# A one-core hybrid decoder trunk: every fourth weight piece's low part is subtracted on GpSimd, with five pairs of piece buffers in place of four

## The chip, the cores and the metric

The kernel runs on one core of one Trainium2 chip. A core has five engines with queues of their own: TensorE (PE in the profile, its weight loads PEld), VectorE (DVE), ScalarE (ACT), GpSimd (POOL) and SyncE (SP), which here issues all DMAs. The metric is the device time of one execution in microseconds (us); lower is better.

## The reference

Two decoder layers run over 256 tokens of width 2048, all in float32. Layer 0 mixes tokens by an eight-head retention, layer 1 by a short gated convolution, and each layer ends with a SwiGLU feed-forward block of width 5632. Scales, shifts and gates of every block come from a conditioning vector c.

```python
c_act = jax.nn.silu(c)
for i in range(DEPTH):                       # DEPTH = 2
    mod = (c_act @ w_mod[i] + b_mod[i])[:, None, :]
    sh1, sc1, g1, sh2, sc2, g2 = jnp.split(mod, 6, axis=-1)
    h = rms_norm(x, norm1_g[i]) * (1.0 + sc1) + sh1
    y = retention_mixer(h, ...) if i == 0 else short_conv_mixer(h, ...)
    x = x + g1 * y
    h = rms_norm(x, norm2_g[i]) * (1.0 + sc2) + sh2
    a, b = jnp.split(h @ ffn_w_in[i], 2, axis=-1)
    x = x + g2 * ((jax.nn.silu(a) * b) @ ffn_w_out[i])
return rms_norm(x, final_g)
```

Nearly all of the work is in the products with the weights: `ret_w_in` (2048 x 12288), `ret_w_out` (4096 x 2048), `conv_w_in` (2048 x 6144), `conv_w_out` (2048 x 2048), and twice `ffn_w_in` (2048 x 11264) and `ffn_w_out` (5632 x 2048).

## The kernel before, in words

**Split products.** Every float32 product is made of three matmuls in a shorter float32 form (fp32r): a value is written as a high part `hi` (a rounded copy) and a low part `lo` (the value less `hi`), and hi x hi, hi x lo and lo x hi are summed in PSUM. Where weights are the stationary side (`product`, lines 447 and 450) the first two of these go in one matmul of 512 columns, the third is one of 256. Where the tokens are the stationary side (`thrice`, lines 460 to 462, used by `by_token` and `sevens`) there are three matmuls of 512 columns.

**Blocks and pieces.** The host lays all weights out in `w_all`, in the order of use, as 456 blocks of 128 x 2048 float32 (1 MB). `fetch` (line 370) issues one DMA on SP into one of `RAW_BUFS = 3` raw buffers; the 192 modulation rows of `w_mod` go through buffers too, most of them through the same three. `prepare` (line 376) makes one piece of a block ready: ScalarE casts the piece to `hi` (line 402), then VectorE subtracts to get `lo` (line 405). An ordinary block has two pieces of 1024 columns, piece 0 (first half) and piece 1 (second half). In the last feed-forward block some pairs of row tiles are multiplied with seven products in place of eight (class `Seven`, function `sevens`). Such a block has four pieces, numbered 2 to 5; VectorE also makes differences of weights for them (lines 391, 395 and 397), and piece 5 is only 512 columns wide. There are 996 pieces in all.

**Who sets the order.** `take` (line 410) hands the next 128 or 512 columns of a piece to the matmuls. When it begins a piece, it drops the one before and calls `prepare` until the piece in use and `AHEAD` further ones are ready in program order (`AHEAD + 1` in the last feed-forward block, line 1394). `hi` and `lo` have `PART_BUFS = 4` buffers each, so the cast of a piece waits until TensorE has finished the piece four before it. The order on TensorE is the program's own. In the start, up to the end of the first spans of the retention input, VectorE and ScalarE follow the program too; after that a scheduler orders VectorE, ScalarE, GpSimd and SP by priorities and estimated times. `units[0]` counts the 128 x 128 weight tiles used so far, in the steps in which `paced` is called; `early` (line 337) is its value behind those first spans.

**Other work beside it.** VectorE also reduces each modulation row against c (lines 318 and 755), adds up and gates the results, and builds the normalised rows of `h` as pairs of high and low parts. GpSimd has only tiny operations: it adds the bias to the modulation results (lines 323 to 328) and takes the power of the mean squares for the norms (line 546) and at the end (lines 1220 to 1222 and 1256).

**Stages**, by the profile's time: retention input and heads to about 780 us, feed-forward of layer 0 to about 1500, convolution to about 1880, the last feed-forward block to the end. The seven-product blocks begin at about 1937 us.

Of the kernel before, what the change touches and what calls it, by code (L numbers as in the profile page):

```python
# [10 lines left out]
F32 = mybir.dt.float32  # L11
# [3 lines left out]
ALU = mybir.AluOpType  # L15
# [26 lines left out]
LAST_TILES = 20, 24  # L42
STORE_AT, LOAD_AT = 0, 2
LEAD_RET, LEAD_CONV, LEAD_FFN = 6, 4, 2
AHEAD = 2
MOD_LEAD = 64
MOST = 0.045
MOD_PRIO = -300
STEPS = (8, 8, 20)
RAW_BUFS = 3  # L50
PART_BUFS = 4
LEFT, ENDS, EARLIER = 8, 2, 120

Q0, K0, V0, G0 = 0, HEADS * DK, 2 * HEADS * DK, 2 * HEADS * DK + HEADS * DV
# [202 lines left out]
def trunk(ctx: ExitStack, tc: tile.TileContext, x_in, c_in, pos_in, w_mod, cols_in, gain_in, tab_in, w_all, out):  # L257
    nc = tc.nc
    const = ctx.enter_context(tc.tile_pool(name="const", bufs=1))
    work = ctx.enter_context(tc.tile_pool(name="work", bufs=2))  # L260
    wpool = ctx.enter_context(tc.tile_pool(name="wpool", bufs=PART_BUFS))
    ps = ctx.enter_context(tc.tile_pool(name="ps", bufs=8, space=PSUM))
# [3 lines left out]
    def name(s):  # L266
        serial[0] += 1
        return f"{s}_{serial[0]}"
# [68 lines left out]
    early = sum(g.n * len(g.ks) for g in RET_SPANS)  # L337
    plan_mod = [(early, 0), (1024, 18), (1984, 49), (5184, n_mod)]
    units, allowed = [0], [0.0]
# [30 lines left out]
    def fetch():  # L370
        raw = wpool.tile([P, CHUNK], F32, tag="raw", name=name("raw"), bufs=RAW_BUFS)
        nc.sync.dma_start(raw, w_all[n_fetched[0]])
        n_fetched[0] += 1
        fetched.append(raw)

    def prepare(between=None):
        if prepared[0] == len(pieces):
            return
        _, piece = pieces[prepared[0]]
        prepared[0] += 1  # L380
        if piece in (0, 2):
            if not fetched:
                fetch()
            raws[:] = [fetched.pop(0)]
            while first <= units[0] < early and len(fetched) < RAW_BUFS - 1 and n_fetched[0] < w_all.shape[0]:
                fetch()
        whole = raws[0]
        b = [whole[:, i : i + DV] for i in range(0, CHUNK, DV)]
        raw = whole[:, :HALF] if piece in (0, 4) else whole[:, HALF:]
        if piece == 2:  # L390
            nc.vector.tensor_tensor(differences, whole[:, DV : 3 * DV], whole[:, : 2 * DV], op=ALU.subtract)
        elif piece == 3:
            raw = differences
        elif piece == 4:
            nc.vector.tensor_tensor(b[1], b[2], differences[:, :DV], op=ALU.subtract)
        elif piece == 5:
            nc.vector.tensor_tensor(b[3], b[3], b[1], op=ALU.subtract)
            raw = b[3]
        width = raw.shape[1]
        hi = wpool.tile([P, HALF], F32R, tag="hi", name=name("hi"))[:, :width]  # L400
        lo = wpool.tile([P, HALF], F32R, tag="lo", name=name("lo"))[:, :width]
        nc.scalar.copy(hi, raw)  # L402
        if between:
            between()
        nc.vector.tensor_tensor(lo, raw, hi.bitcast(F32), op=ALU.subtract)  # L405
        ready.append((hi, lo, width))

    prepared, ahead_now = [0], [AHEAD]

    def take(group, k, col, width=P):  # L410

        assert order.pop() == (group, k, col, width)
        i = place[0] or 0
        if i == 0:
            if place[0] == 0:
                ready.pop(0)
            while len(ready) < 1 + ahead_now[0] * (units[0] >= first):
                n = len(ready)
                prepare()
                if len(ready) == n:  # L420
                    break
        place[0] = (i + width) % ready[0][2]
        return [t[:, i : i + width] for t in ready[0][:2]]
# [255 lines left out]
    with ExitStack() as inner:  # L679
# [64 lines left out]
        with tc.tile_pool(name="start", bufs=1) as sp:  # L744
# [59 lines left out]
            with tc.manual_schedule(engines={mybir.EngineType.DVE, mybir.EngineType.Activation}):  # L804
# [61 lines left out]
                def before(k):  # L866
                    low = []
                    prepare(lambda: low.append(row(k)))
                    low[0]()

                pts = packed(RET_SPANS[0], h, before=before, between=both_reduced, banks=banks)
                prepare()
                prepare()
                for i, pt in enumerate(pts):
# [283 lines left out]
    def made_in_sums():  # L1158

        tmp("beside_sums", (P, BESIDE_SUMS), bufs=1)  # L1160
        for tag, n in (("u", 3), ("low", 3), ("sum", 4)):
            single_sums.extend(tmp(tag, (P, 2, P), F32R, bufs=n) for _ in range(n))
        for i in IN_SEVEN:
            both = tmp("u512", (P, 2, S), pool=mpool, bufs=3)
            for n in range(2):
                k = 2 * i + n
                high, low = [h[k].bitcast(F32)[:, v, :] for v in range(2)]
                nc.vector.tensor_tensor(both[:, n, :], high, low, op=ALU.add)
            in_sums[i] = [single_sums.pop() for _ in range(3)]
            tokens_sums_of(*parts(both), h[2 * i][:, :, P:], in_sums[i])  # L1170
# [217 lines left out]
    for part in range(2):  # L1388
        n = LAST_TILES[part] // 2
        mid = mids(LAST_TILES[part]) if part else first_mid  # L1390
        if not part:
            first_rows(mid[-2:])
            made_in_sums()
            ahead_now[0] = AHEAD + 1
        for i, groups in enumerate(LAST_IN[part]):
# [43 lines left out]
```

## Time and profile before

| what | value |
| --- | --- |
| time, median of 3 runs | 2592.86 us (2591.23 to 2596.55) |
| span of the profiled execution | 2591.5 us; the profile gives no other time for it, so what lies around the span is read from the runs: their median is 1.4 us longer |
| busy: TensorE, VectorE, ScalarE, GpSimd | 2563.3, 2197.4, 1306.0, 125.9 us |
| low-part subtractions on VectorE | 996 (912 + 42 of 1024 columns, 42 of 512) |
| clock granted to TensorE, mean | 0.998 of full speed |
| DMA | 689.56 MB, 266 GB/s on average |

How to read it: a row of the profile names the line of the kernel, the engine, the operation, its output and inputs by tile name (`lo<-raw,hi`), and the shapes. Busy time counts an engine as busy while any of its instructions is under way. Behind a bar or in brackets stands how long the engine idled before the instruction and which instruction ended that idle time. TensorE's matmuls overlap, and their ends are modelled. Spans on GpSimd are rough.

### The profile page before, as it was taken

What the parts mean: (1) busy time and instruction counts of PE and PEld (TensorE: products, weight loads), DVE (VectorE), ACT (ScalarE), POOL (GpSimd) and SP (SyncE); (2) the same over time, 40 slices, a digit from 0 to 9 for tenths busy, and PEclk for the clock granted to TensorE, in tenths of its full rate; (3) what the DMA queues carried; (4) which work ended last, traced back from release to release, by engine and by line L of the source; (5) the groups of instructions that cost most, each with busy time, mean ns of one, the idle gap of its engine ahead of it and who ended that gap; (6) DMA issues with size and microseconds to landing.
All of it is one profiled execution on the core that took longest, in us unless ns stands there. A gap on an engine that the chain in (4) does not pass through costs nothing.

```text
span 2591.5 us, 36408 instructions
## 1 busy us (share of the span) xinstructions
PE 2563.3 (99%) x14181; PEld 2236.3 (86%) x14181; DVE 2197.4 (85%) x2762; ACT 1306.0 (50%) x1792; POOL 125.9 (5%) x232
## 2 busy tenths in 40 slices
PE   7999999999999999999999999999999999999998
PEld 6898889888889888888888898888998888888887
DVE  7988978787698887777778889988989998999978
ACT  5544543444456545334444454444565554556554
POOL 0000000110000000100001001000000000000001
PEclk9999999999999999999999999999999999999999
DMA  9975768767676888777877768877845565555654
GB/s 398 388 293 209 268 243 306 300 248 277 251 282 246 330 323 307 301 296 298 298 294 283 298 237 313 330 297 277 308 165 210 188 223 205 180 210 187 222 208 147
DMA packets 96688, 689.56 MB, mean 266 GB/s; under 512 B 10737, under 2 KB 12161, under 8 KB 13441
## 3 DMA queue, kind: packets, MB, share of 16 engines
q1 hardware_dynamic: 96514, 687.23, 71.3%
q8 instruction: 111, 1.82, 0.3%
q14 instruction: 63, 0.52, 0.1%
HBM read 685.08 MB, written 2.11 MB: 265 GB/s over the span
## 4 chain that ended last, share of the span: by engine, by line
PE 94%; DVE 3%; DMA 2%; issue 1%; ACT 1%; ACTq 0%; POOLq 0%; POOL 0%; DVEq 0%
PE bank L447 30%; PE bank L450 16%; PE bank L461 12%; PE bank L460 12%; PE bank L462 12%; PE bank L495 2%; PE bank L496 2%; PE bank L494 2%; PE bank L627 1%; PE bank L629 1%; PE bank L628 1%; DVE raw L755 1%; DMA raw<-w_all 1%; DVE lo L405 1%; PE bank L983 1%
## 5 line engine op out<-in xcount | busy, mean ns | idle before, releaser
L402 ACT CAST hi<-raw 128x1024 fp32r<-128x1024 f32 (+1 forms) x954 | 978.9, 1033 | 1015.8 <-PE bank L447 346.4
L405 DVE TENSOR_TENSOR lo<-raw,hi 128x1024 fp32r<-128x1024 f32 (+1 forms) x954 | 1133.9, 1197 | 322.6 <-ACT hi L402 317.3
L447 PE MATMUL bank<-h,hi 128*128 128x512 f32 x2016 | 699.3, 390 | 0.0
L450 PE MATMUL bank<-h,lo 128*128 128x256 f32 x2016 | 568.5, 282 | 0.0
L447 PEld LDWEIGHTS bank<-h,hi 128*128 128x128 f32 x2016 | 378.4, 188 | 79.2
L460 PE MATMUL bank<-hi,h 128*128 128x512 f32 x1032 | 405.0, 392 | 2.2 <-DVE rm L739 2.2
L461 PE MATMUL bank<-lo,h 128*128 128x512 f32 x1032 | 404.3, 392 | 0.0
L462 PE MATMUL bank<-hi,h 128*128 128x512 f32 x1032 | 402.7, 390 | 0.0
L450 PEld LDWEIGHTS bank<-h,lo 128*128 128x128 f32 x2016 | 381.0, 189 | 0.1
L318 DVE SCALAR_TENSOR_TENSOR raw<-raw,cb 128x2048 f32<-128x2048 f32 x160 | 365.5, 2284 | 15.7 <-DMA raw<-w_mod 15.3
L447 PE MATMUL bank<-mid,hi 128*128 128x512 f32 x922 | 319.8, 390 | 0.0
L450 PE MATMUL bank<-mid,lo 128*128 128x256 f32 x922 | 260.1, 282 | 0.4 <-DVE lo L405 0.4
L460 PEld LDWEIGHTS bank<-hi,h 128*128 128x128 f32 x1032 | 194.4, 188 | 40.7 <-DVE rm L739 2.8
L462 PEld LDWEIGHTS bank<-hi,h 128*128 128x128 f32 x1032 | 194.2, 188 | 40.8
L461 PEld LDWEIGHTS bank<-lo,h 128*128 128x128 f32 x1032 | 194.5, 188 | 40.4 <-DVE lo L405 3.3
L447 PEld LDWEIGHTS bank<-mid,hi 128*128 128x128 f32 x922 | 173.1, 188 | 36.2
L450 PEld LDWEIGHTS bank<-mid,lo 128*128 128x128 f32 x922 | 174.2, 189 | 0.7 <-DVE lo L405 0.7
L447 PE MATMUL bank<-rm,hi 128*128 128x512 f32 x496 | 172.5, 390 | 0.0
L496 PE MATMUL bank<-h,lo 128*128 128x256 f32 x512 | 146.4, 286 | 4.6 <-DVE lo L405 4.6
L494 PE MATMUL bank<-h,hi 128*128 128x256 f32 x512 | 146.1, 285 | 3.4 <-ACT h L783 3.4
L495 PE MATMUL bank<-h,hi 128*128 128x256 f32 x512 | 146.1, 285 | 0.7 <-DVE h L784 0.7
L450 PE MATMUL bank<-rm,lo 128*128 128x256 f32 x496 | 139.8, 282 | 0.0
(256 smaller groups left out, 3197.4 us busy)
## 6 DMA issues: line engine op xcount, KB each, us to landing
raw<-w_all SPq DMA_DIRECT2D x456, 1024.0 KB, 4.8
raw<-w_mod SPq DMA_DIRECT2D x192, 1024.0 KB, 5.2
x<-x_in SPq DMA_DIRECT2D x4, 512.0 KB, 5.3
out<-xt SPq DMA_DIRECT2D x4, 512.0 KB, 3.0
decay<-tab_in SPq DMA_DIRECT2D x8, 128.0 KB, 2.4
x<-gate_row SPq DMA_DIRECT2D x2, 512.0 KB, 4.8
last_gain<-gain_in SPq DMA_DIRECT2D x1, 1024.0 KB, 7.2
cols<-cols_in SPq DMA_DIRECT2D x1, 152.0 KB, 8.3
```

Source lines behind the costliest of these rows:

```text
L318: nc.vector.scalar_tensor_tensor(raw, raw, 1.0, cb, op0=ALU.mult, op1=ALU.mult, accum_out=total)
L402: nc.scalar.copy(hi, raw)
L405: nc.vector.tensor_tensor(lo, raw, hi.bitcast(F32), op=ALU.subtract)
L447: nc.tensor.matmul(pt, hi, h, start=fresh and k == g.ks[0], stop=False, skip_group_check=True)
L450: nc.tensor.matmul(pt[:, 1, :], lo, h[:, 0, :], start=False, stop=last and k == g.ks[-1], skip_group_check=True)
L460: nc.tensor.matmul(o, hi, w_hi, start=first, stop=False)
L461: nc.tensor.matmul(o, hi, w_lo, start=False, stop=False)
L462: nc.tensor.matmul(o, lo, w_hi, start=False, stop=last)
L494: nc.tensor.matmul(pt, hi, h[:, 0, :], start=first, stop=False, skip_group_check=True)
L495: nc.tensor.matmul(pt, hi, h[:, 1, :], start=False, stop=False, skip_group_check=True)
L496: nc.tensor.matmul(pt, lo, h[:, 0, :], start=False, stop=last, skip_group_check=True)
L627: nc.tensor.matmul(pt, hi, high, start=k == 0, stop=False, skip_group_check=True)
```

## The change

Three constants or options and one line of `prepare` change.

- The low part is subtracted on GpSimd, not on VectorE, if the piece is the second half of an ordinary block (`piece == 1`), the first spans are over (`units[0] >= early`), and the number of pieces prepared so far, this one included, is a multiple of four. That is 192 of the 996 pieces. Inputs, output and arithmetic are the same.
- `PART_BUFS` goes from 4 to 5: one more pair of `hi` and `lo` buffers, 8 KB of each partition.
- `AHEAD` goes from 2 to 3, and with it from 3 to 4 in the last feed-forward block.
- `dynamic_dma_scratch_size=1024` makes the memory that is kept for DMAs issued by GpSimd smaller, which gives room for the fifth pair. The kernel issues no such DMA.

Behind the changed line, all later lines of the kernel move down by one.

```diff
-AHEAD = 2
+AHEAD = 3
...
-PART_BUFS = 4
+PART_BUFS = 5
...
         nc.scalar.copy(hi, raw)
         if between:
             between()
-        nc.vector.tensor_tensor(lo, raw, hi.bitcast(F32), op=ALU.subtract)
+        other = units[0] >= early and piece == 1 and prepared[0] % 4 == 0
+        (nc.gpsimd if other else nc.vector).tensor_tensor(lo, raw, hi.bitcast(F32), op=ALU.subtract)
         ready.append((hi, lo, width))
...
-    nc = bacc.Bacc("TRN2", target_bir_lowering=False, num_devices=1)
+    nc = bacc.Bacc("TRN2", target_bir_lowering=False, num_devices=1, dynamic_dma_scratch_size=1024)
```

## The prediction

> **What bounds the kernel now.** I read the head of the page first, then the busy time of each engine in stretches of 100 us, then the waits of TensorE.
>
> ```profile
> span 2591.5 us, 36408 instructions
> PE 2563.3 (99%) x14181; PEld 2236.3 (86%) x14181; DVE 2197.4 (85%) x2762; ACT 1306.0 (50%) x1792; POOL 125.9 (5%) x232
> ```
>
> ```profile
> 0.00:100.00 100.00, 84.46 (x462) 70.12 (x463) 84.23 (x92) 59.36 (x95) 1.57 (x5) 1.00 0.98 397
> 100.00:200.00 100.00, 97.83 (x614) 88.33 (x613) 86.88 (x99) 46.74 (x62) 0.00 (x0) 0.98 0.79 312
> ...
> 1200.00:1300.00 100.00, 100.00 (x579) 88.67 (x578) 77.86 (x93) 48.75 (x73) 5.67 (x10) 1.00 0.80 295
> ...
> 1600.00:1700.00 100.00, 100.00 (x578) 88.66 (x578) 90.07 (x123) 45.49 (x61) 5.14 (x13) 1.00 0.87 329
> ...
> 2300.00:2400.00 100.00, 100.00 (x448) 82.19 (x447) 94.40 (x115) 59.56 (x71) 0.00 (x0) 1.00 0.54 192
> 2500.00:2600.00 100.00, 82.56 (x364) 67.76 (x362) 71.07 (x87) 42.64 (x55) 8.02 (x8) 0.96 0.42 148
> ```
>
> The columns are stretch, length, then PE, weight loads, DVE, ACT and POOL, each with its instructions. TensorE idles 28.2 us of the span (2591.5 less 2563.3). 15.5 us lie in the first 100 us, 2.2 in the next 100, and about 9 in the tail (82.56 of the 91.5 us that the span leaves there). So hardly 2 us are left over the 2300 us in between, whether VectorE is 78% or 94% busy: 579 matmuls per 100 us at 78%, 578 at 90%. VectorE is loaded, but it isn't the bound. The waits of TensorE after the first 100 us are few enough to be listed (us in total, times, longest):
>
> ```profile
> PE bank L460 <- DVE rm L739: 2.2, 2, 1.4
> PE bank L461 <- DVE lo L405: 0.5, 1, 0.5
> PE bank L983 <- DVE sp L512: 0.5, 1, 0.5
> PE bank L450 <- DVE lo L405: 0.4, 1, 0.4
> ```
>
> Relief for VectorE can therefore win next to nothing. What it can lose is the question: a low half that comes later than TensorE needs it.
>
> **Part 1: 192 subtractions leave VectorE.** In the instruction order of the changed kernel 192 of the 996 low-part subtractions stand on GpSimd, all 128x1024, one in four pieces from about 205 us on: 9 in 100 us up to 1900, 41 after 1930. Their price on VectorE is the first row here:
>
> ```profile
> L405 DVE TENSOR_TENSOR lo<-raw,hi 128x1024 fp32r<-128x1024 f32 x912 | 1107.2, 1221 | 315.9 <-ACT hi L402 310.8
> ```
>
> ```profile
> L323 POOL TENSOR_SCALAR mcol<-msum,cols x48: 288/401/3314, 426.4 to 1583.9; 128x1 f32<-128x1 f32 x48
> L546 POOL TENSOR_TENSOR rs<-rs,half x11: 688/711/1559, 237.4 to 1879.9; 128x2 f32<-128x2 f32 x11
> L544 DVE TENSOR_SCALAR rs<-bank x3: 150/155/158, 785.9 to 1879.7; 128x2 f32<-128x2 f32 x3
> ```
>
> VectorE loses 192 x 1.2 = 230 us of work. I cost that at 0 us of span: TensorE's own stream covers it, as the windows show.
>
> **Part 2: what one costs on GpSimd.** No row has a wide operation there. Lower end: 1.22 us, VectorE's own time. Between the tiny operations of the two engines the ratio is 288 ns to 155 (tensor_scalar, shortest against median), so 1.9, up to 711 to 155 (the power), so 4.6. That gives 1.22 x 1.9 = 2.3 us and 1.22 x 4.6 = 5.6 us. I take 2.3, since a subtraction is nearer the plain row than the power, and keep 1.22 and 5.6 for the range. The Trainium skill, page "GPSIMD Engine Reference", section "Elementwise — side-by-side cycle accounting", gives 4497 ns for 2048 columns; half of it, an estimate of 2.25 us, would lower the sum below by 0.5 us; no row here shows it.
>
> **Part 3: GpSimd waits for VectorE before it starts.** The same 128x1 operation takes 288 ns or over 1 us. The timeline tells why:
>
> ```profile
> 1015.32 1.22 DVE L405 TENSOR_TENSOR lo<-raw,hi 128x1024 fp32r<-128x1024 f32 x1
> ```
>
> ```profile
> 1015.50 1.19 POOL L323 TENSOR_SCALAR mcol<-msum,cols 128x1 f32<-128x1 f32 x1 [9.10 <-DVE raw L318]
> 2539.79 4.43 POOL L1220 TENSOR_TENSOR sums<-total 128x1 f32<-128x1 f32 x1 [659.15 <-ACT u L1370]
> ```
>
> ```profile
> 2538.87 1.22 DVE L405 TENSOR_TENSOR lo<-raw,hi 128x1024 fp32r<-128x1024 f32 x1
> 2540.01 0.68 DVE L1371 TENSOR_TENSOR xt<-xt,last_gain 128x512 f32<-128x512 f32 x1
> 2540.61 1.22 DVE L391 TENSOR_TENSOR x<-raw 128x1024 f32<-128x1024 f32 x1
> 2541.75 0.68 DVE L405 TENSOR_TENSOR lo<-raw,hi 128x512 fp32r<-128x512 f32 x1
> 2542.35 0.68 DVE L395 TENSOR_TENSOR raw<-raw,x 128x512 f32<-128x512 f32 x1
> 2542.95 2.35 DVE L405 TENSOR_TENSOR lo<-raw,hi 128x1024 fp32r<-128x1024 f32 x2
> ```
>
> The first GpSimd operation ends at 1016.69, 0.15 us behind the VectorE subtraction that ran when it began. The second sits through five VectorE operations in a row, all with both inputs in SBUF, and ends at 2544.22, as the sixth does (2542.95 plus half of 2.35). So a GpSimd subtraction will wait for VectorE's stretch of two-SBUF-input work to let it in. The longest wait on record is 4.43 less the 0.19 to 0.29 that such an operation needs, so 4.2 us; the shortest is 0.
>
> **Part 4: the fifth pair and pieces three ahead (four in the last stage).** A piece's high half can be cast when the pair that it reuses is free, now five pieces back, not four. In ordinary matmul stages a piece is 16 matmuls, 16/579 of 100 us = 2.76 us. From then to its use are four pieces: 11.0 us, less 1.05 for the cast, 4.2 for the longest wait and 2.3 for the operation leaves 3.4 us. So nothing is late before 1930 us. At 5.6 us per operation the same piece is still in time, by 0.1 us.
>
> In the last stage it is tighter. An ordinary piece is 12 matmuls (12/448 of 100 us = 2.7 us), but the four pieces of a seven-product block are 6, 6, 6 and 3 matmuls (1.3, 1.3, 1.3 and 0.7 us), and VectorE makes differences there too. A moved piece that is the second half of a lone ordinary block behind a seven-product block has only 1.3 + 1.3 + 0.7 + 2.7 = 6.0 us of lead. Following the moved pieces through the rows of casts and first uses, I find nine of these too short, the first at 1953 and the last at 2538 us. The casts of the first, of the one used at 2314 (its own at 2309.28, the one before it at 2307.97) and of the last; then VectorE's stretch at 2310; then the first uses of the three:
>
> ```profile
> 1947.94 1.06 ACT L402 CAST hi<-raw 128x1024 fp32r<-128x1024 f32 x1 [0.26 <-PE bank L462]
> ...
> 2307.97 1.06 ACT L402 CAST hi<-raw 128x1024 fp32r<-128x1024 f32 x1 [0.47 <-ACT hi L402]
> 2309.28 1.06 ACT L402 CAST hi<-raw 128x1024 fp32r<-128x1024 f32 x1 [0.26 <-PE bank L462]
> ...
> 2533.00 2.20 ACT L402 CAST hi<-raw 128x1024 fp32r<-128x1024 f32 x2
> ```
>
> ```profile
> 2310.13 3.49 DVE L405 TENSOR_TENSOR lo<-raw,hi 128x1024 fp32r<-128x1024 f32 x3
> ```
>
> ```profile
> 1952.95 0.39 PE L461 MATMUL bank<-lo,h 128*128 128x512 f32 x1
> ...
> 2314.25 0.39 PE L461 MATMUL bank<-lo,h 128*128 128x512 f32 x1
> ...
> 2537.52 0.39 PE L461 MATMUL bank<-lo,mid 128*128 128x512 f32 x1
> ```
>
> Here the cast starts at 2309.28, and with a fifth pair one short piece (1.3 us) earlier, so its end moves from 2310.34 to 2309.0. VectorE then goes on without a gap (three subtractions from 2310.13 alone last to 2313.62). 2309.0 + 4.2 + 2.3 = 2315.5, against a first use at 2314.25: 1.3 us late. The nine together, reckoned alike, are 12.4 us late (1.2 to 1.8 each). At 1.22 us per operation they are 2.7 us late; with no wait none is; at 5.6 us they are 9 x 3.3 us more, 42 us in all.
>
> The same lead helps where pieces were late at the start, before any subtraction is moved:
>
> ```profile
> 42.98 0.39 PE L496 MATMUL bank<-h,lo 128*128 128x256 f32 x1 [0.76 <-DVE lo L405]
> 46.33 0.39 PE L496 MATMUL bank<-h,lo 128*128 128x256 f32 x1 [0.26 <-DVE lo L405]
> 50.27 0.39 PE L496 MATMUL bank<-h,lo 128*128 128x256 f32 x1 [0.87 <-DVE lo L405]
> ```
>
> ```profile
> 41.70 1.23 DVE L405 TENSOR_TENSOR lo<-raw,hi 128x1024 fp32r<-128x1024 f32 x1 [4.73 <-ACT hi L402]
> ```
>
> VectorE idles 4.73 us for a cast, which had no free pair; with a fifth it makes that piece within the gap and stays one ahead: -1.9 us (between 0, if rows of h then come as late, and -1.9).
>
> **Part 5: what moves with it, at nothing.** The scratch of GpSimd's own DMAs shrinks; every issue in the page is on SP. The moved operation also frees the raw buffer, for which the next load waits:
>
> ```profile
> SPq L372 <- DVE lo L405: 576.8, 118, 10.6
> ```
>
> ```profile
> raw<-w_all SPq DMA_DIRECT2D x456, 1024.0 KB, 4.8
> ```
>
> Every second block's buffer comes free 1.1 us later by the operation and up to 4.2 by the wait. Before 1930 the 3.4 us of spare lead hide most of it; if they don't, about 1 us a time. GpSimd's small operations stay in order between the subtractions; the three norm roots stand four pieces behind the subtraction ahead of them in its order, so they lose nothing, or at most 2.3 + 4.2 us each where it is late.
>
> **Sum.** Against the profiled execution's span of 2591.5: -1.9 + 12.4 = 2602.0 us. The median of the runs shown, 2592.86, is 1.4 us above that span, so 2603.4.
>
> **Rivals.**
> Hidden anyway: GpSimd gets in at the next boundary between two VectorE operations (a wait up to 1.2 us), which the row at 1015.50 fits and the one at 2539.79 does not. Even with waits up to 2.2 us all nine are in time. Then only -1.9 to 0 stays: 2591 to 2593.
> VectorE becomes the bound: the blocking goes both ways, so that VectorE stands while GpSimd reads for 2.3 us. No operation here is long enough to show that. The last stage is where it would count:
>
> ```profile
> 1930.00:2560.00 630.00, 629.46 (x2808) 518.94 (x2808) 569.49 (x670) 353.76 (x407) 5.38 (x2) 1.00 0.56 201
> ```
>
> 39 of the 41 fall in it: 569.5 - 39 x 1.2 + 39 x 2.3 = 612 of 630 us, against 60 us idle before. In the densest 100 us, 94.40 + 6 x 1.1 = 101. If VectorE's idle, which waits for casts, cannot move, all 39 x 1.1 = 43 us land on TensorE, at the other end 1 us; half, 22 us, on top of the forecast gives 2625, all of it 2646. It decides from about 2.0 us per operation. The Trainium skill says this in "SBUF — State Buffer", section "Who interferes with whom": of a VectorE instruction with two SBUF inputs and a GpSimd one that reads SBUF, the second to issue blocks until the first ends. The rows above bear out half of it (4.43 us for 0.19); the other half no run here shows.
> Faster: nothing is late and the remaining waits go too: -1.9 - 2.2 - 0.5 - 0.4 = -5.0, so 2587.9. One place decides it, the wait for the rm sums (2.2 us near 120 and 160 us): VectorE must reach them sooner, against which speaks that it is at 86.88 of 100 us there and no subtraction is moved before 205.
>
> **Numbers.** About 0.2% (5.2 us) is what a measurement of this kernel can tell from no change. Forecast 0.43; VectorE the bound 0.25; hidden 0.25; faster 0.07. So slower 0.68, same 0.25, faster 0.07. The forecast's own range is 2597 to 2620. The range 2589.5 to 2648 takes in the hidden case and most of the second rival; it leaves out the faster one and operations near 5.6 us.
>
> **What would show it.** Right: GpSimd subtractions of 2.3 us or more, with waits up to 4 us in the last stage; TensorE waits for GpSimd's lo at L461, 1 to 2 us each, about nine, all after 1930; none before. Second rival: VectorE subtractions with a mean well above 1221 ns and many small TensorE waits for VectorE's lo. Wrong: no waits for GpSimd at all, or waits in the 800 to 1900 us stretch, where I have 3.4 us to spare; a GpSimd subtraction above 5 us would do that.

## The result, and the profile after

The changed kernel takes 2671.86 us (median of 4 runs, 2668.34 to 2674.11), the kernel before 2592.27 us beside it: a ratio of 1.0303 with a 95% interval of 1.0289 to 1.0318. It is slower, as forecast, but by 80 us, not 11, and the time lies outside the range given.

The head of the page of the changed kernel (its profiled execution took 2668.34 us):

```profile
span 2666.2 us, 36668 instructions
PE 2587.5 (97%) x14181; PEld 2247.7 (84%) x14181; DVE 2204.8 (83%) x2570; ACT 1290.9 (48%) x1792; POOL 665.2 (25%) x424
```

Two things stand out. TensorE idles 78.7 us (28.2 before), and is busy 24.2 us longer for the same 14181 matmuls. And VectorE, which gave away 192 subtractions, is busy no less than before (2197.4). Less the 192 x 1.221 us it should be busy 1963.0; the other 241.8 us are 1.26 us for each subtraction on GpSimd.

Where the time went, in stretches; first the kernel before, then the changed one (columns as above: PE, weight loads, DVE, ACT, POOL, then clock, DMA share, GB/s):

```profile
200.00:800.00 600.00, 599.42 (x3421) 528.36 (x3420) 491.82 (x639) 281.92 (x391) 42.78 (x74) 1.00 0.71 266
800.00:1900.00 1100.00, 1099.58 (x6587) 984.87 (x6586) 917.66 (x1182) 529.03 (x763) 73.54 (x145) 1.00 0.79 295
1900.00:2500.00 600.00, 599.46 (x2744) 496.85 (x2744) 545.72 (x668) 346.34 (x427) 0.00 (x0) 1.00 0.56 200
```

```profile
200.00:800.00 600.00, 586.84 (x3273) 513.31 (x3272) 467.86 (x566) 270.41 (x375) 181.07 (x121) 0.99 0.70 258
800.00:1900.00 1100.00, 1072.70 (x6316) 950.10 (x6317) 887.54 (x1030) 491.54 (x729) 338.46 (x236) 1.00 0.76 283
1900.00:2500.00 600.00, 594.92 (x2875) 502.07 (x2874) 550.40 (x650) 342.77 (x435) 108.95 (x44) 0.99 0.56 203
```

In the first two stretches TensorE idles 13.2 and 27.3 us, where it idled 0.6 and 0.4 before; from 1900 to 2500 it is 5.1. So most was lost where the prediction had nothing late: the first difference of weights for the seven-product blocks (L391) begins at 1930.6 us in the trace of before and 64 us later, at 1994.2 us, in that of the changed kernel. TensorE's longest waits in the changed kernel, as a list (total, times, longest):

```profile
PE bank L451 <- DVE lo L406: 14.2, 21, 1.5
PE bank L495 <- ACT h L784: 5.8, 3, 3.0
PE bank L533 <- ACT acc L519: 5.8, 2, 3.0
PE bank L448 <- ACT hi L402: 5.6, 7, 1.3
PE bank L1004 <- DVE o L993: 5.4, 2, 3.5
PE bank L628 <- DVE h L615: 4.7, 1, 4.7
PE bank L451 <- POOL lo L406: 4.5, 7, 1.1
PE bank L462 <- POOL lo L406: 3.8, 1, 3.8
```

GpSimd's own low halves account for 8.3 us in eight waits. Far more is lost waiting for VectorE: for low halves that it still makes (L451), for rows of the retention output (L1004) and for the shift row (L628). The norm sums (L533) come from ScalarE, but before the stall that ends at 1941.90 ScalarE had itself idled 4.27 us for a row from VectorE. The casts that L448 waits for are taken up below, with the loads. The row of L495 lies in the start and is the same with the pairs alone. The two engines' subtractions (busy, mean ns, idle before them), and two other operations of VectorE with two inputs in SBUF:

```profile
L406 DVE TENSOR_TENSOR lo<-raw,hi 128x1024 fp32r<-128x1024 f32 x720 | 938.1, 1311 | 282.0 <-ACT hi L402 278.4 <-PE bank L451 0.9
L406 POOL TENSOR_TENSOR lo<-raw,hi 128x1024 fp32r<-128x1024 f32 x192 | 529.6, 2758 | 1313.1 <-ACT hi L402 1003.5 <-DVE cos L712 189.8 <-DVE lo L406 55.2
L318 DVE SCALAR_TENSOR_TENSOR raw<-raw,cb 128x2048 f32<-128x2048 f32 x160 | 418.3, 2615 | 89.0 <-DMA raw<-w_mod 88.6
L1067 DVE TENSOR_TENSOR m<-sum,silu 128x256 f32<-128x256 f32 x44 | 41.2, 936 | 1.1
```

By tile, with the shortest, median and longest GpSimd operation in ns:

```profile
L406 POOL TENSOR_TENSOR lo<-raw,hi x192: 2337/2474/4518, 205.2 to 2645.0; 128x1024 fp32r<-128x1024 f32 x192
```

The same on VectorE before (its subtraction stood at 1221 ns):

```profile
L318 DVE SCALAR_TENSOR_TENSOR raw<-raw,cb 128x2048 f32<-128x2048 f32 x160 | 365.5, 2284 | 15.7 <-DMA raw<-w_mod 15.3
L1066 DVE TENSOR_TENSOR m<-sum,silu 128x256 f32<-128x256 f32 x44 | 18.5, 420 | 0.5
```

The timeline of the changed kernel shows what stretches them. GpSimd, then VectorE:

```profile
934.56 4.08 POOL L406 TENSOR_TENSOR lo<-raw,hi 128x1024 fp32r<-128x1024 f32 x1 [6.17 <-ACT hi L402]
...
959.39 2.41 POOL L406 TENSOR_TENSOR lo<-raw,hi 128x1024 fp32r<-128x1024 f32 x1 [2.98 <-ACT hi L402]
```

```profile
776.56 4.10 DVE L318 SCALAR_TENSOR_TENSOR raw<-raw,cb 128x2048 f32<-128x2048 f32 x1
...
934.08 2.28 DVE L318 SCALAR_TENSOR_TENSOR raw<-raw,cb 128x2048 f32<-128x2048 f32 x1
...
936.74 2.18 DVE L1067 TENSOR_TENSOR m<-sum,silu 128x256 f32<-128x256 f32 x1
...
960.83 3.12 DVE L318 SCALAR_TENSOR_TENSOR raw<-raw,cb 128x2048 f32<-128x2048 f32 x1 [1.77 <-DMA raw<-w_mod]
```

At 936.74 VectorE begins an operation that takes 0.42 us alone. It ends at 938.92, 0.28 us behind the end of GpSimd's subtraction (938.64). GpSimd itself had first waited for the VectorE reduction that ran until 936.36. At 960.83 the reduction begins under a GpSimd subtraction that lasts until 961.80, and ends 2.15 us after that, about its own length. So each engine stands while the other reads. The Trainium skill, page "SBUF — State Buffer", section "Who interferes with whom", says that whichever of two such instructions issues second blocks until the first ends; this trace now bears out both halves of it.

The loads suffer as well: the casts of before, then those of the changed kernel, and there the modulation rows and SP, which waits for the buffers that GpSimd frees:

```profile
ACT hi L402 <- DMA raw<-w_all: 179.9, 88, 6.0
```

```profile
ACT hi L402 <- DMA raw<-w_all: 452.7, 172, 8.1
DVE raw L318 <- DMA raw<-w_mod: 88.6, 74, 3.8
SPq L372 <- POOL lo L406: 350.1, 123, 8.7
SPq L310 <- POOL lo L406: 116.6, 39, 5.6
```

Last, the clock. Behind the longer stalls TensorE restarts at half of it (windows of the changed kernel: 3.5 us behind the stall that ends at 330.73, and the stretch behind the one that ends at 1941.90):

```profile
331.00:334.50 3.50, 3.50 (x13) 3.11 (x12) 3.46 (x6) 0.74 (x2) 0.00 (x0) 0.50 0.17 28
1942.00:1948.80 6.80, 6.80 (x38) 6.80 (x38) 4.14 (x5) 3.17 (x4) 1.62 (x1) 0.61 0.81 288
```

The mean granted clock is 0.993, against 0.998 before. 0.007 x 2666.2 less 0.002 x 2591.5 is 13.5 us of the 24.2 us of longer busy time, though both figures are rounded to the third digit. Added up over windows of 0.5 us, each with its own busy time and clock, it is 15.4 us less 1.6, so 13.8. The other 10 us aren't explained here.

### The profile page after: what moved, and what is told of

Same layout as the page of the kernel before. It is cut to its first block, busy times and chain, and to the rows that moved or that the text cites. A ratio compares the mean times of both kernels' runs of the same rounds, so it can differ in the third digit from the quotient of the medians.

```text
span 2666.2 us, 36668 instructions
## 1 busy us (share of the span) xinstructions
PE 2587.5 (97%) x14181; PEld 2247.7 (84%) x14181; DVE 2204.8 (83%) x2570; ACT 1290.9 (48%) x1792; POOL 665.2 (25%) x424
## 3 DMA queue, kind: packets, MB, share of 16 engines
q8 instruction: 111, 1.82, 0.3%
## 4 chain that ended last, share of the span: by engine, by line
PE 53%; DMA 11%; DVE 9%; issue 6%; POOL 4%; ACT 3%; ACTq 0%; POOLq 0%; SPq 0%; DVEq 0%
PE bank L448 12%; PE bank L462 9%; PE bank L463 9%; PE bank L461 9%; DMA raw<-w_all 8%; PE bank L451 6%; POOL lo L406 4%; DMA raw<-w_mod 3%; DVE lo L406 3%; ACT hi L402 3%; DVE raw L318 3%; PE bank L628 1%; PE bank L630 1%; PE bank L629 1%; PE bank L497 1%
## 5 line engine op out<-in xcount | busy, mean ns | idle before, releaser
L402 ACT CAST hi<-raw 128x1024 fp32r<-128x1024 f32 (+1 forms) x954 | 969.0, 1031 | 896.5 <-DMA raw<-w_all 452.7
L406 DVE TENSOR_TENSOR lo<-raw,hi 128x1024 fp32r<-128x1024 f32 x762 | 966.5, 1279 | 283.4 <-ACT hi L402 279.7
L406 POOL TENSOR_TENSOR lo<-raw,hi 128x1024 fp32r<-128x1024 f32 x192 | 529.6, 2758 | 1313.1 <-ACT hi L402 1003.5
L448 PE MATMUL bank<-h,hi 128*128 128x512 f32 x2016 | 701.6, 391 | 4.4 <-ACT hi L402 4.3
L451 PE MATMUL bank<-h,lo 128*128 128x256 f32 x2016 | 570.8, 283 | 13.4 <-DVE lo L406 10.4
L318 DVE SCALAR_TENSOR_TENSOR raw<-raw,cb 128x2048 f32<-128x2048 f32 x160 | 418.3, 2615 | 89.0 <-DMA raw<-w_mod 88.6
L448 PEld LDWEIGHTS bank<-h,hi 128*128 128x128 f32 x2016 | 378.5, 188 | 85.0 <-ACT hi L402 6.6
L462 PE MATMUL bank<-lo,h 128*128 128x512 f32 x1032 | 404.9, 392 | 1.9 <-DVE lo L406 1.9
L451 PEld LDWEIGHTS bank<-h,lo 128*128 128x128 f32 x2016 | 380.8, 189 | 20.7 <-DVE lo L406 15.8
L448 PE MATMUL bank<-mid,hi 128*128 128x512 f32 x922 | 320.4, 390 | 1.1 <-ACT hi L402 1.0
L451 PE MATMUL bank<-mid,lo 128*128 128x256 f32 x922 | 260.8, 283 | 4.8 <-DVE lo L406 3.0
L462 PEld LDWEIGHTS bank<-lo,h 128*128 128x128 f32 x1032 | 195.3, 189 | 40.4 <-DVE lo L406 3.0
L448 PEld LDWEIGHTS bank<-mid,hi 128*128 128x128 f32 x922 | 173.1, 188 | 37.7 <-ACT hi L402 1.8
L451 PEld LDWEIGHTS bank<-mid,lo 128*128 128x128 f32 x922 | 174.2, 189 | 7.3 <-DVE lo L406 4.9
L448 PE MATMUL bank<-rm,hi 128*128 128x512 f32 x496 | 172.7, 391 | 0.2 <-ACT hi L402 0.2
L495 PE MATMUL bank<-h,hi 128*128 128x256 f32 x512 | 146.9, 287 | 6.2 <-ACT h L784 5.8
L497 PE MATMUL bank<-h,lo 128*128 128x256 f32 x512 | 146.7, 287 | 2.5 <-DVE lo L406 2.5
```

The costliest lines, as they stand in the source:

```text
L318: nc.vector.scalar_tensor_tensor(raw, raw, 1.0, cb, op0=ALU.mult, op1=ALU.mult, accum_out=total)
L406: (nc.gpsimd if other else nc.vector).tensor_tensor(lo, raw, hi.bitcast(F32), op=ALU.subtract)
L448: nc.tensor.matmul(pt, hi, h, start=fresh and k == g.ks[0], stop=False, skip_group_check=True)
L451: nc.tensor.matmul(pt[:, 1, :], lo, h[:, 0, :], start=False, stop=last and k == g.ks[-1], skip_group_check=True)
L462: nc.tensor.matmul(o, hi, w_lo, start=False, stop=False)
L495: nc.tensor.matmul(pt, hi, h[:, 0, :], start=first, stop=False, skip_group_check=True)
```

## The experiments

Each edit is shown against the changed kernel, except the last of the third group, which is given against the kernel before. The kernel before, run beside them, took 2592.4 to 2593.5 us.

**First group: the parts of the change, and the buffers.** The pairs without GpSimd's subtractions:

```diff
-        other = units[0] >= early and piece == 1 and prepared[0] % 4 == 0
+        other = False
```

> The changed kernel with all subtractions left on VectorE: five pairs of piece buffers, pieces three ahead. Theory A (GpSimd is the cause, by either way below): 2588 to 2593 us, as before, with the three waits for lo at 43 to 50 us gone. Rival C (the order with pieces three ahead makes loads or rows late): 2620 us or more.

Measured: 2594.83 us, 1.0010 (1.0001 to 1.0019). The fifth pair and the longer lead are worth nothing: 2 us slower, hardly to be told from no change.

GpSimd's subtractions without the pairs:

```diff
-AHEAD = 3
+AHEAD = 2
-PART_BUFS = 5
+PART_BUFS = 4
```

> 192 subtractions on GpSimd, four pairs of buffers, pieces two ahead as before. Theory A: as slow as the changed kernel or slower, 2672 to 2720 us, since a piece has 2.8 us less lead. Rival C: most of the loss is gone, under 2630 us.

Measured: 2682.66 us, 1.0352 (1.0337 to 1.0367). The whole loss comes from the subtractions on GpSimd; the pairs take 11 us of it back.

First halves on GpSimd, so that VectorE stays the last to read the raw buffer (191 operations):

```diff
-        other = units[0] >= early and piece == 1 and prepared[0] % 4 == 0
+        other = units[0] >= early and piece == 0 and prepared[0] % 4 == 3
```

> The changed kernel, but GpSimd takes the first half of every second ordinary block and VectorE the second, so that GpSimd's operation is not the last reader of the raw buffer. As many operations on GpSimd. Theory A1 (the raw buffer is held longer, so loads start late): 2590 to 2620 us, and ScalarE's waits for weight loads fall from 453 us towards the 180 of before. Theory A2 (VectorE is held while GpSimd reads): 2655 to 2690 us, VectorE's mean subtraction stays near 1311 ns against 1221.

Measured: 2639.62 us, 1.0189 (1.0173 to 1.0204). 32 us go when GpSimd isn't the last reader, 45 over the pairs alone stay, and the casts wait as long for loads (472.8 us). That is neither of the two outcomes, so it isn't only that GpSimd hands the buffer back late.

A fourth raw buffer, in room that the scratch of GpSimd's unused DMAs gives:

```diff
-RAW_BUFS = 3
+RAW_BUFS = 4
...
-dynamic_dma_scratch_size=1024
+dynamic_dma_scratch_size=256
```

> The changed kernel with a fourth raw buffer (and 256 bytes of scratch for GpSimd's DMAs, of which there are none). Theory A1: 2590 to 2610 us. Theory A2: GpSimd still holds VectorE as long (mean subtraction near 1311 ns), but if that costs time through the loads only, the time falls as well, to 2600 to 2625; if it costs time by making low parts and rows late, it stays above 2645 us.

Measured: 2617.62 us, 1.0099 (1.0085 to 1.0113). 54 of the 80 us are gone, and with them most of the casts' waits, while VectorE's subtraction is still stretched (one row of the waits, one of the groups):

```profile
ACT hi L402 <- DMA raw<-w_all: 53.4, 23, 6.7
```

```profile
L406 DVE TENSOR_TENSOR lo<-raw,hi 128x1024 fp32r<-128x1024 f32 x720 | 982.4, 1373 | 152.7 <-ACT hi L402 150.4
```

**Second group: do the reads collide, and where does it cost?** The pairs and a fourth raw buffer, nothing on GpSimd (the two edits `other = False` and `RAW_BUFS = 4`):

> The control for the fourth raw buffer: five pairs, pieces three ahead, four raw buffers, no subtraction on GpSimd. If the fourth buffer only gives back what GpSimd takes: 2588 to 2596 us, no faster than before. If the kernel before was itself short of raw buffers: under 2585 us.

Measured: 2587.66 us, 0.9979 (0.9969 to 0.9988): faster than both kernels. So with four raw buffers GpSimd's subtractions cost 30 us, with three 77 (2671.9 less 2594.8).

All low parts on VectorE, and 192 further subtractions on GpSimd whose result nothing uses:

```diff
-        other = units[0] >= early and piece == 1 and prepared[0] % 4 == 0
+        other = False
...
+        if units[0] >= early and piece == 1 and prepared[0] % 4 == 0:
+            nc.gpsimd.tensor_tensor(spare, spare, spare, op=ALU.subtract)
```

> All 996 subtractions stay on VectorE, with five pairs, pieces three ahead and three raw buffers; beside them GpSimd does 192 subtractions of a 128x1024 scratch tile from itself, at the same places, for which nobody waits and which read no raw buffer. Theory A2 (VectorE is held while GpSimd reads): VectorE's mean subtraction rises by 100 ns or more over 1223 and the time to 2610 to 2680 us. If GpSimd only holds buffers and makes low parts late (A1 alone): 2588 to 2600 us, with VectorE's mean at 1225.

Measured: 2874.47 us, 1.1084 (1.1065 to 1.1102). Since they depend on nothing, the scheduler put all 192 back to back into the first 520 us, not at the pieces' places. So the run doesn't price the change, but it shows the collision by itself: 282 us for 192 operations that read SBUF.

The same with an operation that writes but reads nothing (the edit is against the run just told of; here too all 192 went to the start):

```diff
-            nc.gpsimd.tensor_tensor(spare, spare, spare, op=ALU.subtract)
+            nc.gpsimd.memset(spare, 0.0)
```

> As the run with the extra subtractions, but GpSimd sets the scratch tile to zero, so that it reads nothing. If the reads are what collides: 2588 to 2598 us, VectorE's mean subtraction at 1225 ns. If any wide GpSimd operation holds VectorE: as slow as the extra subtractions.

Measured: 2593.03 us, 1.0006 (0.9997 to 1.0016). No effect. VectorE's subtraction in the two runs, with GpSimd's operation:

```profile
L406 DVE TENSOR_TENSOR lo<-raw,hi 128x1024 fp32r<-128x1024 f32 x912 | 1216.8, 1342 | 294.8 <-ACT hi L402 283.0 <-PE bank L452 2.9 <-PE bank L455 1.9
L408 POOL TENSOR_TENSOR spare<-spare 128x1024 f32<-128x1024 f32 x192 | 500.2, 2605 | 15.0
```

```profile
L406 DVE TENSOR_TENSOR lo<-raw,hi 128x1024 fp32r<-128x1024 f32 x912 | 1106.9, 1222 | 308.0 <-ACT hi L402 300.4 <-PE bank L455 1.2
L408 POOL MEMSET spare<- 128x1024 f32 x192 | 183.5, 956 | 11.0
```

GpSimd's reads hold VectorE up; its writes and its mere being busy don't. The section "Who interferes with whom" of the Trainium skill's page "SBUF — State Buffer" draws the line there, too.

Only the subtractions of the last stage on GpSimd (41):

```diff
-        other = units[0] >= early and piece == 1 and prepared[0] % 4 == 0
+        other = prepared[0] > 664 and piece == 1 and prepared[0] % 4 == 0
```

> The changed kernel, with GpSimd's subtractions in the last feed-forward block alone (the 41 pieces after about 1930 us). By the forecast that nine of these are late there: 2603 to 2612 us, with TensorE waits for GpSimd's lo of 1 us and more. By theory A1 (loads, which the last stage has to spare: no cast waits for a load there before): 2590 to 2600 us.

Measured: 2603.44 us, 1.0039 (1.0024 to 1.0054), 8.6 us over the pairs alone. That is in the range of the first outcome, but not by its nine late pieces. It leaves some 68 of the 77 us for the 151 subtractions ahead of the last stage. One wait for GpSimd's low half is all there is in it (L462, 3.8 us). The changed kernel has the same one:

```profile
2600.08 6.72 POOL L1221 TENSOR_TENSOR sums<-total 128x1 f32<-128x1 f32 x1 [17.92 <-ACT u L1371]
2606.75 2.34 POOL L406 TENSOR_TENSOR lo<-raw,hi 128x1024 fp32r<-128x1024 f32 x1
```

```profile
2609.15 0.56 PE L462 MATMUL bank<-lo,mid 128*128 128x512 f32 x1 [3.81 <-POOL lo L406]
```

The low half takes the least that such an operation takes. It is late because it is queued behind a 128x1 sum of the final norm, which waited 17.92 us for ScalarE and then stood 6.72 us.

**Third group: late buffers and held VectorE apart.** First halves on GpSimd, as above, with a fourth raw buffer:

> First halves of ordinary blocks are subtracted by GpSimd (as in the run that moved first halves, 2639.6 us), now with four raw buffers. Two costs are in dispute for what is left of that run's 45 us over the pairs-only kernel (2594.8). If the loads' buffers carry it even where GpSimd is not the last reader (VectorE, held while GpSimd reads, then gives the buffer back late), the fourth buffer takes most of it: 2600 to 2620, and the casts' waits for loads fall from 473 us to under 100. If it is VectorE held, late for rows and norm sums whatever the buffers do, it stays at 2630 to 2640.

Measured: 2614.57 us, 1.0085 (1.0072 to 1.0099), with 50.7 us of casts' waits for loads: the first outcome, so late buffers were part of it even where VectorE is the last reader. But 27 us over the kernel with four buffers and no such work (2587.66) remain of 45, so here they are the smaller part.

One piece in eight on GpSimd (`prepared[0] % 8 == 0`):

> As the changed kernel, with one in eight pieces on GpSimd in place of one in four (96 subtractions, not 192). If each subtraction costs its share (VectorE held 1.2 us and the buffer given back late each time), half the loss over the pairs-only kernel remains: 2594.8 + 77/2 = 2633. If what costs is that delays pile up where there is no slack between two of them, far less remains, 2600 to 2615. If the loss is a property of having GpSimd in the chain of the buffers at all, nearly all of it remains, over 2650.

Measured: 2621.67 us, 1.0109 (1.0096 to 1.0123). Half the operations cost 27 of the 77 us, between the first two outcomes: 0.28 us for each of its 97, 0.53 for each of the other 95. The casts wait 391.9 us for loads here already, so the loss isn't in proportion to that sum.

The raw buffer held about 2 us longer at the same places, by an operation that reads nothing:

```diff
-        other = units[0] >= early and piece == 1 and prepared[0] % 4 == 0
-        (nc.gpsimd if other else nc.vector).tensor_tensor(lo, raw, hi.bitcast(F32), op=ALU.subtract)
+        nc.vector.tensor_tensor(lo, raw, hi.bitcast(F32), op=ALU.subtract)
+        if units[0] >= early and piece == 1 and prepared[0] % 4 == 0:
+            nc.gpsimd.memset(raw, 0.0)
+            nc.gpsimd.memset(raw, 0.0)
```

> All subtractions on VectorE; where the changed kernel gives one to GpSimd, GpSimd instead overwrites the half of the raw buffer just used, twice (memset, 956 ns each where it was measured; the buffer isn't read any more, so nothing that is computed changes). It reads nothing, so VectorE should not be held, but the buffer comes free about 2 us later, 192 times. If the late buffers alone make the loss (VectorE's subtraction stays at about 1222 ns), the time is 2630 to 2670 and the casts wait 300 us or more for loads. If the late buffers cost only together with a held VectorE, it is 2594 to 2610.

Measured: 2609.81 us, 1.0067 (1.0052 to 1.0082). The waits of this kernel, and VectorE's subtraction:

```profile
ACT hi L402 <- DMA raw<-w_all: 426.5, 202, 8.6
SPq L372 <- POOL raw L408: 517.3, 144, 8.9
```

```profile
L405 DVE TENSOR_TENSOR lo<-raw,hi 128x1024 fp32r<-128x1024 f32 x912 | 1099.9, 1221 | 323.5 <-ACT hi L402 314.6 <-PE bank L453 2.2 <-PE bank L450 0.8
```

SP waits longer for GpSimd than in the changed kernel (517.3 us against 350.1), the casts wait nearly as long for loads, and VectorE is undisturbed: that alone costs 15 us over the pairs, 22 over the same kernel with four raw buffers (2587.66). The time lies at the upper edge of the second outcome, though the casts wait as the first one had it. So a late buffer is mostly absorbed as long as VectorE is free.

The kernel before with a fourth raw buffer and nothing else (`RAW_BUFS = 4` and a scratch of 1024):

> The kernel before with a fourth raw buffer alone (four pairs, pieces two ahead, nothing on GpSimd). With five pairs and three ahead the fourth buffer gave 2587.7, 5 us under before. If that gain comes from the buffer, it stays here: 2586 to 2589. If it needs the fifth pair as well, 2591 to 2593.

Measured: 2588.57 us, 0.9983 (0.9974 to 0.9991). The 4 to 5 us come from the buffer, not from the pairs, and this is the smallest edit that beats both kernels. Its casts wait 17.1 us for loads, not 179.9.

**Fourth group: what was left.** A sixth pair, pieces four ahead, three raw buffers:

```diff
-AHEAD = 3
+AHEAD = 4
-PART_BUFS = 5
+PART_BUFS = 6
...
-dynamic_dma_scratch_size=1024
+dynamic_dma_scratch_size=256
```

> The changed kernel with a sixth pair of piece buffers and pieces four ahead, in the space that a fourth raw buffer took in the other run (2617.6). If the moved low halves are late for want of lead counted in pairs (as the prediction counted it), a piece more of lead, about 2.8 us, takes as much off as the fourth raw buffer did, 2610 to 2630. If the casts wait for loads and so cannot use a further pair, it stays at 2660 to 2675 and the casts' waits for loads are 430 us or more.

Measured: 2640.12 us (2632.52 to 2647.43), 1.0187 (1.0170 to 1.0204): neither outcome. 32 us are recovered although the casts wait still longer for loads (498.6 us). A piece more of lead absorbs part of the lateness, a raw buffer in the same room more (2617.62).

Four raw buffers, all low halves on VectorE, and at the moved pieces' places a GpSimd subtraction that reads (it overwrites the half that is no longer needed):

```diff
+            nc.gpsimd.tensor_tensor(raw, hi.bitcast(F32), hi.bitcast(F32), op=ALU.subtract)
```

(in the place of the two memsets above, with `RAW_BUFS = 4`)

> Four raw buffers, all low halves on VectorE; at the places where the changed kernel moves one, GpSimd afterwards subtracts the high half from itself into the raw half that is no longer needed (nothing that is computed uses it). So no low half waits for GpSimd, but GpSimd reads SBUF as often as in the changed kernel, and VectorE keeps the work of the 192. With four raw buffers the changed kernel had 2617.6, without GpSimd's subtractions 2587.7. If most of these 30 us is VectorE held while GpSimd reads, this run is at 2610 or more (more than the changed kernel's share is possible, since VectorE has 234 us more to do). If they come from the low half being ready later through GpSimd's longer operation, it is 2588 to 2598.

Measured: 2654.64 us, 1.0238 (1.0218 to 1.0258), 67 us over the same kernel without those reads. No low half comes from GpSimd here. The two longest rows of TensorE's waits, the casts' waits, and VectorE's subtraction:

```profile
PE bank L452 <- DVE lo L405: 19.9, 27, 1.5
PE bank L629 <- DVE h L616: 5.9, 1, 5.9
ACT hi L402 <- DMA raw<-w_all: 116.3, 49, 6.6
```

```profile
L405 DVE TENSOR_TENSOR lo<-raw,hi 128x1024 fp32r<-128x1024 f32 x912 | 1221.9, 1353 | 99.5 <-ACT hi L402 97.3
```

So GpSimd can cost this much while it delivers nothing that TensorE waits for: VectorE is held (1353 ns on average, 1221 without the reads). But GpSimd also writes into the raw buffer here and gives it back later, and the casts wait 116.3 us for loads against 15.5 without the reads, so the 67 us aren't the price of the reads alone. Nor is it the changed kernel with one thing taken out, since VectorE keeps 234 us of work. The 37 us over the 2617.62 of the run with four raw buffers suggest that, once the reads are there, taking the 192 subtractions off VectorE helps, and that the reads cost more than that. No run separates this from the buffer that comes later.

No run rules out one rival: a scheduler orders VectorE's work, and each kernel has an order of its own. Of VectorE's some 1770 instructions other than these subtractions, the longest list that runs in the same order in the changed kernel and in the pairs alone has some 1660, that in the pairs alone and the kernel before some 1580. So the pairs alone changed the order more than the subtractions did, and cost 2 us; a new order is an unlikely cause of the 77.

## Why the prediction was wrong

Direction and bound were right: TensorE sets the time, and the change is slower. The fifth pair was put at -1.9 to 0 us and brings nothing: in the start the waits for low halves at L497 fell from 4.6 to 2.6 us, near the 1.9 forecast, but those for h rose by 2.4. The size was wrong, because of two steps that were each costed on their own, at nothing ahead of 1930 us.

- **Part 4, "nothing is late before 1930 us"**, is the step that failed. In place of 0 us, the 151 subtractions ahead of the last stage cost some 68. It counted 11.0 us of lead from the pairs alone and put against it only GpSimd's own operation and wait. Two things were missing. A cast needs its load as well, and already before 88 casts waited for theirs, up to 6.0 us; that row was not used. And the low halves that stay on VectorE come later when GpSimd holds it: TensorE waited 14.2 us for those at L451, and 4.5 us there for GpSimd's own.
- **Part 5, the raw buffer that comes free later, "at nothing"**: alone it costs 15 us (buffers held, VectorE free). The row shown for it, 576.8 us, is that of 1900 to 2550 us only; over the whole span SP waits 1107.4 us for VectorE's low halves at L372, 264 times. "About 1 us a time" for 192 times would have been far too much; nothing was too little.
- **The rival "VectorE becomes the bound"** had the right mechanism, in the wrong place and by the wrong measure. It was allowed for the last stage only, where VectorE is busiest, and priced by VectorE's busy time against its idle time. There the change costs 8.6 us. Ahead of that stage VectorE had idle time enough, and the time went all the same. A held operation is late for whoever waits for it: a raw buffer, a norm sum, a shift. The 4.70 us stall at 800 us is an example. Its shift row needs modulation sums that VectorE reduces. One of them took 4.10 us at 776.56 against 2.28 alone. The last began only at 795.71, in VectorE's queue behind a low half that was held (1.82 us at 791.71) and whose cast had waited 1.73 us for its load; how much of the stall each made isn't shown. Measured, VectorE is held 1.26 us per subtraction (2.3 was taken as the whole).
- **The two together** are what no step had. With four raw buffers, GpSimd's subtractions cost 30 us; late buffers without reads cost 15; with three buffers and the reads it is 77. That they draw on the same few microseconds of lead, and that each alone is partly absorbed by it, fits this and the runs with a piece of lead less (11 us more) and a piece more (32 us less). It is argued, not shown: how the 32 us beyond the sum of the two are made up stall by stall wasn't resolved.
- **Part 1, relief for VectorE worth 0**: VectorE was busy no less, so there was no relief. Where VectorE is held anyway, the relief may be worth something: 37 us by the last run, which differs in more than that.
- **Part 2, 2.3 us per operation**: right. The shortest took 2.34, the median 2.47, the mean is 2.76. The Trainium skill's figure, which gave an estimate of 2.25 ("GPSIMD Engine Reference", "Elementwise — side-by-side cycle accounting"), agrees within 4% for an operation that isn't held.
- **Part 3, waits of up to 4.2 us**: too long for a wide operation. The longest took 4.52, so waited 2.2, and on average 0.4. It was read from a 128x1 sum, and that sum is indeed starved again, for 6.72 us.
- **Nine pieces late after 1930, 12.4 us**: one was, by 3.81 us, and behind that sum. For the others the rival "hidden" was right: waits up to 2.2 us leave them in time. That the last stage costs 8.6 us, near these 12.4, is luck.
- **The clock** was in no step: some 13.5 us, by the half-clock stretches at the new stalls.

Of what was named to show the prediction wrong, "waits in the 800 to 1900 us stretch" came true, but not by a slow GpSimd. And "VectorE subtractions with a mean well above 1221 ns and many small TensorE waits for VectorE's lo", named for the second rival, is what the profile shows.

## What to carry to other kernels

Before work goes to GpSimd, list what VectorE runs at that time: here its operations with two inputs in SBUF and GpSimd's operations that read SBUF took turns, so that VectorE was busy no less after giving away 192 of 2762 instructions. Count the lead of a pipeline from its latest input, loads included, and only once: two delays that are each mostly absorbed alone can overrun the lead together (here 15 and 30 us, measured in two different kernels, stand against 77). The casts' waits for loads in the profile of before pointed to a cheaper use of the space: a fourth raw buffer in place of the fifth pair makes the kernel 0.17% faster.

## What the runs showed of the hardware that was not expected

TensorE's clock fell to half at stalls of under 3 us, and stayed there for 3.4 or 6.8 us. Four stalls in the timeline of the changed kernel, a window at half clock around the end of the first, and the windows behind the two short ones (those behind the other two stand above):

```profile
330.73 0.66 PE L1004 MATMUL bank<-tab,o 128*128 128x128 f32 x2 [3.49 <-DVE o L993]
537.88 0.90 PE L1004 MATMUL bank<-tab,o 128*128 128x128 f32 x5 [1.93 <-DVE o L993]
1941.90 0.59 PE L533 MATMUL bank<-ones,acc 128*128 128x1 f32 x2 [2.78 <-ACT acc L519]
2018.25 0.50 PE L462 MATMUL bank<-lo,h 128*128 128x512 f32 x1 [1.91 <-DVE lo L406]
```

```profile
329.60:336.00 6.40, 5.27 (x17) 4.53 (x18) 6.13 (x9) 0.90 (x3) 0.20 (x1) 0.50 0.30 100
538.00:541.40 3.40, 3.40 (x19) 2.81 (x19) 3.33 (x6) 0.00 (x0) 1.30 (x1) 1.00 0.25 67
2018.20:2021.60 3.40, 3.35 (x9) 2.68 (x10) 3.37 (x4) 1.05 (x1) 0.00 (x0) 0.61 0.61 205
```

At the stall of 3.49 us the clock falls before TensorE restarts: in windows of 0.4 us it is halved from about 329.5 to 336.3 us. At that of 2.78 us it is halved from about 1940.4 to 1947.3 us, at that of 1.91 us from 2018.9 to 2022.3 us, 0.7 us after the restart. At that of 1.93 us it isn't lowered at all. The Trainium skill, page "TensorE: Matmul & The Clock Gate", section "Why this matters for your kernels", gives idle gaps of about 3 us as the limit; here shorter ones were enough at times, and what tells them apart the runs don't show. 3.4 us of busy time at half the clock lose 1.7 us on top of the stall. The changed kernel has eight such stretches ahead of its last matmul, two of them of 6.8 us, the kernel before has one.
